# Selection of the sparse branch with two small operations per bit and new planner lengths; attention's two output parts stored apart

## The chip, the cores and the metric

The kernel runs on one core of a Trainium2 chip. A core has five engines with queues of their own: TensorE (PE in the profile; its weight loads are PEld), VectorE (DVE), ScalarE (ACT), GpSimd (POOL) and SyncE (SP), which here only starts transfers. The metric is the device time of one execution in microseconds (us).

## What is computed

One layer of a decoder trunk on 1024 tokens of width 1024. Three groups of 8 attention heads run side by side: A (sparse: an indexer scores all keys, each query keeps its 256 best), B (forgetting) and C (stick-breaking). Their outputs are projected, gated and summed, projected once more, and a layer norm, an MLP and a second layer norm follow. Cut to the two places of the change:

```python
score = einsum('bqhk,bqh->bqk', relu(dots), wb)          # indexer, 16 heads
score = where(causal, score, -inf)
_, idx = top_k(score, 256)                               # branch A: keys kept per query
...
branches = stack([o_a, o_b, o_c])                        # (3, b, s, 512)
up = einsum('ibsw,iwd->bsid', branches, w_branch)
merged = sum(up * sigmoid(gates), axis=2)
```

## The kernel before

Products of fp32 matrices are made from split operands: a tile is cut into a high and a low part, and three matmuls (high-high, high-low, low-high) give one product. In the first 1223 us the core makes the input projections and gates (`Dense`, whose results lie in three PSUM banks with the tag `d`), the indexer's scores, and then three times 8 heads of attention, in the order B (`Fox`), C (`Stick`), A (`Dsa`). A head has 4 units of two blocks of 128 queries; a unit makes its rows (`qk`), transposes the probabilities block by block (`tr`, 240 in all, 80 per branch; each ends on DVE with the subtraction `pl<-t,ph`) and multiplies them with the values (`pv`). Each `Stick` row needs a scan of the whole row on DVE (`u<-u,zero`).

**The selection.** `select` (L683) finds, for 6 blocks of 128 queries, the 256th largest score by bisection over the 32 bits of a float. For each bit DVE counts in each block how many scores reach the candidate (`count`, 6 operations `jk<-sc,fb` of 384 to 1024 columns) and then updates the candidate with operations on 128x6 values. After the last bit one more round counts, and 5 operations per block (`eq`, `rk`, `eq`, `eq`, `sc`; below "the ranking") turn the scores into distances or a large number for keys that are not kept. Branch A reads these.

**Who orders the work.** The program is written once, in an order that a planner chooses. `Plan.account` (L109) keeps a clock for each engine and adds to it the length that `_Engine` (L121) ascribes to each operation. `drive` (L753) emits the next piece of attention that is ready by these clocks, or else a step of the dense projections, which may run ahead of attention by two blocks of heads (`dense_upto`, L853). The selection is a generator that runs in the background: `fill_gap` (L95) emits pieces of it wherever DVE's planned clock has a gap of more than 0.8 us, up to a budget that grows with the transposes done (`bg_allowed`, L871), by the three numbers `BG`:

```python
while more and until - self.t["DVE"] > BG_GAP and self.bg_done < self.bg_allowed():
...
def bg_allowed():
    f = 3.0 * st["tr"] / len(trs)
    return BG[0] + (BG[1] - BG[0]) * f if f < 1.0 else BG[1] + (BG[2] - BG[1]) * (f - 1.0)
```

Each piece reports its length by `yield`, and the sum of these is `bg_done`. When the first rows of branch A come up and the selection isn't over, `next_attention` (L831) emits all that is left at once.

**The output of attention.** `Unit.pv` (L651) collects 512 queries of a head in one PSUM bank of 128 rows: 64 rows from the high and 64 from the low part of the values. ACT copies the two halves to SBUF, POOL adds them, and a transfer of 64x512 stores them to `o_scratch`. In the branch stage `load_o` (L890) brings 4 tiles of 128x1024 per branch back, and ACT and DVE split each.

Of the kernel before, what the change touches and what calls it, by code (L numbers as in the profile page):

```python
# [13 lines left out]
F32 = mybir.dt.float32  # L14
F32R = mybir.dt.float32r
BF16 = mybir.dt.bfloat16
I32 = mybir.dt.int32
# [28 lines left out]
FORGET = (13, 37)  # L46
X1_AT = 6


BG = (5.0, 95.0, 185.0)  # L50
BG_GAP = 0.8
# [69 lines left out]
class _Engine:  # L121
# [5 lines left out]
    def __getattr__(self, op):  # L127
        f = getattr(self.eng, op)

        def call(*args, **kw):  # L130
# [12 lines left out]
            if self.name == "T":  # L143
                eng, us = "PE", max(0.107, 0.000422 * n)
                if op == "matmul" and ins[0].dtype == BF16:
                    us = 0.056
            elif self.name == "V":
                fast = not psum and op in ("tensor_copy", "tensor_scalar") and "accum_out" not in kw
                eng, us = "DVE", 0.07 + n / (1920 if fast else 960)
            elif self.name == "A":  # L150
                eng, us = "ACT", (0.05 if psum else 0.09) + n / 1200
                if "accum_out" in kw:
                    us += 0.15
            elif self.name == "G":
                eng, us = "POOL", 0.06 + n * (0.0023 if op == "tensor_tensor" else 0.00106)
            else:
                size = n * out[0].shape[0] * 4
                eng, us, lat = "DMA", size / 340e3, 2.0
# [6 lines left out]
def trunk(ctx: ExitStack, tc: tile.TileContext, x, w_in, b_forget, w_branch, w_out,  # L165
# [269 lines left out]
    def gate(br, e):  # L435
        def evac(b):
            for c, t_ in zip(HALVES, b):
                g_ = plan.tile(dp, [P, 512], F32, tag="o", bufs=3, name="g_")
                A.activation(g_, t_, AF.Copy)
                nc.scalar.dma_start(g_dram[br, e * P:(e + 1) * P, c], g_)  # L440
        return proj_T([(0, win(OGT + br * D + e * P))], evac)
# [33 lines left out]
    def log_sigmoid():  # L475
        n = S * NH // P
        z, t1, t2 = (plan.tile(dp, [P, n], F32, tag="o", bufs=3, name=nm) for nm in ("z", "t1", "t2"))
        e_ = row_tile(7, "e_")[:, :n]
# [129 lines left out]
    class Unit:  # L608
# [42 lines left out]
        def pv(self, jp):  # L651
# [12 lines left out]
            if u % 2 == 1 and jp == u:  # L664
                t_ = plan.tile(dp, [P, 512], F32, tag="o", bufs=3, name="o")
                t2 = plan.tile(dp, [P, 512], F32, tag="o", bufs=3, name="o2")
                A.activation(t_[0:64], k.ob[0:64], AF.Copy)
                A.activation(t2[0:64], k.ob[64:128], AF.Copy)
                G.tensor_tensor(t_[0:64], t_[0:64], t2[0:64], ALU.add)

                q = nc.scalar if k.branch == 0 and h == NH - 1 else Q
                q.dma_start(o_dram[k.branch, h * HD:(h + 1) * HD, HALVES[u // 2]], t_[0:64])


    NI = len(TI)
    ub = cp.tile([P, NI], I32, name="ub")
    cb = cp.tile([P, NI], I32, name="cb")
    fb = cp.tile([P, NI], I32, name="fb")
# [4 lines left out]
    def select():  # L683
        def decode(dst, src):
            V.tensor_scalar(dst, src, 31, -1, op0=ALU.arith_shift_right, op1=ALU.bitwise_xor)
            V.scalar_tensor_tensor(dst, dst, -2 ** 31, src, op0=ALU.bitwise_or, op1=ALU.bitwise_xor)

        def count(cmp):
            for n, i in enumerate(TI):
                jk = plan.tile(ap, [P, S], U8, tag="jk", name="jk")  # L690
                V.tensor_scalar(jk[:, :(i + 1) * P], score[i], fb[:, n:n + 1].bitcast(F32), 0.0,
                                op0=cmp, op1=ALU.add, accum_out=cnt[:, n:n + 1])
                yield (i + 1) * 0.133

        for i in TI:
            G.affine_select(score[i][:, i * P:], score[i][:, i * P:], pattern=[[-1, P]],
                            compare_op=ALU.is_ge, fill=LOWEST, base=0, channel_multiplier=1)
        V.memset(ub, 0)
        for bit in range(31, -1, -1):
            V.tensor_scalar(cb, ub, (1 << bit) - (1 << 32 if bit == 31 else 0), None,  # L700
                            op0=ALU.bitwise_or)
            decode(fb, cb)
            yield from count(ALU.is_ge)
            V.tensor_scalar(mb, cnt, float(TOPK), None, op0=ALU.is_ge)
            V.copy_predicated(ub, mb, cb)
        decode(fb, ub)
        yield from count(ALU.is_gt)
        V.tensor_scalar(need, cnt, -1.0, float(TOPK), op0=ALU.mult, op1=ALU.add)

        for i in TI:  # L710
# [3 lines left out]
            eq = plan.tile(ap, [P, S], U8, tag="jk", name="eq")[:, :w]  # L714
            rk = plan.tile(dp, [P, S], F16, tag="o", bufs=3, name="rk")[:, :w]
            V.tensor_scalar(eq, score[i], thr, None, op0=ALU.is_equal)
            V.tensor_tensor_scan(rk, eq, zeros(P, w), 0.0, ALU.add, ALU.add)
            V.scalar_tensor_tensor(eq, rk, need[:, n:n + 1], eq, op0=ALU.is_le, op1=ALU.mult)
            V.scalar_tensor_tensor(eq, score[i], thr, eq, op0=ALU.is_le, op1=ALU.subtract)
            dist = plan.tile(dp, [P, S], F16, tag="o", bufs=3, name="dist")[:, :w]  # L720
            G.iota(dist, pattern=[[-1, w]], base=i * P, channel_multiplier=1,
                   allow_small_or_imprecise_dtypes=True)
            V.scalar_tensor_tensor(score[i], eq, BIG, dist, op0=ALU.mult, op1=ALU.add)
            yield (i + 1) * 0.7

# [164 lines left out]
    def load_o(n):  # L890
        parts = []
        for t_ in range(4):
            raw = gp.tile([P, S], F32, tag="oraw", bufs=3, name="oraw")
            Q.dma_start(raw, o_dram[branches[n], t_ * P:(t_ + 1) * P, :])
            parts.append((gp.tile([P, S], F32R, tag="oh", bufs=5, name="oh"),
                          gp.tile([P, S], F32R, tag="ol", bufs=5, name="ol")))
            split(*parts[-1], raw)
# [524 lines left out]
```

## Time and profile before

| | us |
|---|---|
| median of 3 runs (lowest, highest) | 2100.05 (2097.78, 2100.82) |
| the profiled execution | 2103.51 |
| its span, first to last instruction | 2101.8 |
| PE busy | 2026.3 (96%) |
| DVE busy | 1448.6 (69%) |
| ACT busy | 1054.0 (50%) |
| POOL busy | 541.5 (26%) |

The busy shares are over the whole span; the stretches that matter here are from 242 us (the first `pl<-t,ph` of attention) to 561 us (the first of branch C's transposes), from there to 862 us (near the end of branch C), from there to 1223 us (end of attention), and the branch stage up to 1420 us.

### The profile page before, as it was taken

Reading aid. Unit: us, or ns where it says so; the run is one execution under the profiler, and the core shown is the slowest. Engines: PE = TensorE matmul, PEld = TensorE weight load, DVE = VectorE, ACT = ScalarE, POOL = GpSimd, SP = SyncE. Lnnn points to the kernel's source line nnn. Section 1 sums busy time; section 2 is a strip of 40 time slices with the busy share of each in tenths; the row PEclk is TensorE's granted clock in tenths of the full one; section 3 lists DMA queues with packets and bytes.
Section 4 is the critical chain, followed back from the end, with each engine's and each line's share of the span. In section 5 each row is a group of like instructions: output and inputs, shape, how many; then the busy total and the mean of one; then the engine's idle time right before and its main releaser. Section 6 shows DMA issues by size and latency. Waiting matters only on the chain.

```text
span 2101.8 us, 29749 instructions
## 1 busy us (share of the span) xinstructions
PE 2026.3 (96%) x10534; PEld 1701.8 (81%) x10534; DVE 1448.6 (69%) x2651; ACT 1054.0 (50%) x2025; POOL 541.5 (26%) x508
## 2 busy tenths in 40 slices
PE   8999999999998998999999999999999999999998
PEld 7888878888877876888988888887787778888886
DVE  3886489788899999545433334766888776785557
ACT  5674455455565364446454443445544445654443
POOL 3212333333454356356445403100000000000003
PEclk9999999999999999999999999999999999999999
DMA  4111322232121221222122355631499945886653
GB/s 129 52 35 47 72 80 69 76 76 69 41 54 41 58 58 36 54 66 78 47 75 79 87 181 183 218 123 56 143 355 329 332 162 174 312 300 191 194 186 120
DMA packets 184277, 264.63 MB, mean 126 GB/s; under 512 B 17192, under 2 KB 109352, under 8 KB 182080
## 3 DMA queue, kind: packets, MB, share of 16 engines
q1 hardware_dynamic: 170144, 237.29, 36.7%
q10 hardware_dynamic: 13984, 25.43, 3.3%
q8 instruction: 83, 1.36, 0.3%
q14 instruction: 66, 0.54, 0.1%
HBM read 176.59 MB, written 73.50 MB: 119 GB/s over the span
## 4 chain that ended last, share of the span: by engine, by line
PE 59%; DVE 15%; DMA 8%; issue 5%; ACT 3%; POOL 1%; SPq 0%; DVEq 0%; ACTq 0%; POOLq 0%
PE d L137 49%; PE o L137 4%; DVE u L137 3%; PE l L137 3%; PE t L137 3%; DMA w2raw<-in_w_ff_dram 3%; DMA t_scratch<-w2raw 2%; DVE jk L137 2%; DVE pl L137 1%; DMA woraw<-in_w_out_dram 1%; DVE mr L137 1%; DMA w1raw<-in_w_ff_dram 1%; DVE w2raw L137 1%; DVE p L137 1%; DVE hl L137 1%
## 5 line engine op out<-in xcount | busy, mean ns | idle before, releaser
L137 PE MATMUL d<-xh,whi 128*128 128x512 f32 (+1 forms) x912 | 316.3, 401 | 17.5 <-DVE qb L137 12.8
L137 PE MATMUL d<-xh,wlo 128*128 128x512 f32 (+1 forms) x912 | 307.4, 393 | 0.0
L137 PE MATMUL d<-xl,whi 128*128 128x512 f32 (+1 forms) x912 | 303.2, 388 | 0.0
L137 PE MATMUL d<-u 128*128 128x512 f32 x1320 | 301.0, 390 | 1.9 <-ACT u L137 1.2
L137 PEld LDWEIGHTS d<-u 128*128 128x128 f32 x1320 | 247.5, 188 | 55.2 <-ACT u L137 2.2
L137 POOL TENSOR_TENSOR wlo<-wraw,whi 128x512 fp32r<-128x512 f32 x138 | 191.5, 1391 | 311.2 <-ACT whi L137 209.4
L137 POOL TENSOR_TENSOR z<-z,res 128x512 f32<-128x512 f32 x14 | 19.7, 1429 | 750.8 <-ACT z L137 747.9
L137 PEld LDWEIGHTS d<-xh,whi 128*128 128x128 f32 x912 | 168.4, 192 | 48.7 <-issue 18.0
L137 DVE TENSOR_TENSOR u<-sr,u 128x512 fp32r<-128x512 f32 x220 | 144.6, 702 | 89.9 <-ACT u L137 89.3
L137 ACT ACTIVATE u<-sr 128x512 fp32r<-128x512 f32 x220 | 130.2, 627 | 140.1 <-PE d L137 103.8
L137 PEld LDWEIGHTS d<-xl,whi 128*128 128x128 f32 x912 | 173.6, 191 | 31.8
L137 DVE TENSOR_TENSOR pl<-t,ph 128x512 fp32r<-128x512 f32 (+1 forms) x240 | 147.7, 630 | 67.0 <-ACT ph L137 65.7
L137 PEld LDWEIGHTS d<-xh,wlo 128*128 128x128 f32 x912 | 166.7, 191 | 27.1
L137 DVE TENSOR_SCALAR_CACHE_REDUCE jk<-sc,fb 128x384 uint8<-128x384 f32 (+2 forms) x198 | 186.2, 941 | 3.4
L137 ACT ACTIVATE whi<-wraw 128x512 fp32r<-128x512 f32 x136 | 86.1, 633 | 187.5 <-PE d L137 128.4
L137 ACT ACTIVATE p<-p,nm 128x128 f32<-128x128 f32 (+7 forms) x128 | 99.3, 776 | 142.4 <-DVE nm L137 129.7
L137 ACT ACTIVATE ph<-t 128x512 fp32r<-128x512 f32 (+1 forms) x240 | 128.0, 555 | 80.9 <-PE t L137 78.9
L137 PE MATMUL o<-pl,v 128*128 128x256 f32 x480 | 122.8, 292 | 20.5 <-DVE pl L137 20.3
L137 POOL TENSOR_SCALAR p<-p,sm 128x128 f32<-128x128 f32 (+7 forms) x128 | 96.1, 752 | 158.1 <-DVE sm L137 140.3
L137 PE MATMUL o<-ph,v 128*128 128x256 f32 x480 | 126.5, 284 | 0.4 <-ACT o L137 0.2
L137 PEld LDWEIGHTS o<-pl,v 128*128 128x128 f32 x480 | 92.2, 192 | 35.0 <-DVE pl L137 30.2
L137 ACT ACTIVATE mr<-mr 128x512 f32<-128x512 f32 x110 | 69.4, 631 | 93.5 <-DVE mr L137 91.8
(285 smaller groups left out, 4618.0 us busy)
## 6 DMA issues: line engine op xcount, KB each, us to landing
wraw<-in_w_in_dram SPq DMA_DIRECT2D x136, 256.0 KB, 2.9
sr<-h_scratch SPq DMA_DIRECT2D x112, 256.0 KB, 3.3
w1raw<-in_w_ff_dram SPq DMA_DIRECT2D x16, 1024.0 KB, 5.7
h_scratch<-mr SPq DMA_DIRECT2D x64, 256.0 KB, 2.4
w2raw<-in_w_ff_dram SPq DMA_DIRECT2D x16, 1024.0 KB, 8.2
t_scratch<-w2raw SPq DMA_DIRECT2D x16, 1024.0 KB, 7.8
sr<-t_scratch SPq DMA_DIRECT2D x64, 256.0 KB, 3.9
sg<-g_scratch SPq DMA_DIRECT2D x24, 512.0 KB, 3.3
```

The source lines that it names most:

```text
L137: r = f(*args, **kw)
```

## The change

It has three parts.

1. The candidate is kept in the form in which it is compared, so that a bit is updated by two operations (`mb`, then `fb`) in place of five (`mb`, `ub`, `cb`, `fb`, `fb`).
2. The planner's lengths for DVE change: operations of under 16 columns 0.2 us and more, scans about twice as long, operations with an accumulator 0.07 us longer. The pieces of the selection report other lengths too, and `BG` becomes (6, 115, 223).
3. The two parts of an attention output are copied in one ACT operation and stored apart by two transfers; POOL's addition goes. `load_o` fetches both parts, 8 tiles in place of 4 per branch (4 buffers, before 3), and DVE adds them ahead of the split.

```diff
-X1_AT = 6
-BG = (5.0, 95.0, 185.0)
+NO = 3
+BG = (6.0, 115.0, 223.0)
...
-                eng, us = "DVE", 0.07 + n / (1920 if fast else 960)
+                eng, us = "DVE", (0.2 if n < 16 else 0.07) + n / (1920 if fast else 960)
+                if op == "tensor_tensor_scan":
+                    us += n / 870
+                elif "accum_out" in kw or op == "tensor_tensor_reduce":
+                    us += 0.07
...
-                t_ = plan.tile(dp, [P, 512], F32, tag="o", bufs=3, name="o")
-                t2 = plan.tile(dp, [P, 512], F32, tag="o", bufs=3, name="o2")
-                A.activation(t_[0:64], k.ob[0:64], AF.Copy)
-                A.activation(t2[0:64], k.ob[64:128], AF.Copy)
-                G.tensor_tensor(t_[0:64], t_[0:64], t2[0:64], ALU.add)
+                t_ = plan.tile(dp, [P, 512], F32, tag="o", bufs=NO, name="o")
+                A.activation(t_, k.ob, AF.Copy)
                 q = nc.scalar if k.branch == 0 and h == NH - 1 else Q
-                q.dma_start(o_dram[k.branch, h * HD:(h + 1) * HD, HALVES[u // 2]], t_[0:64])
+                for part in range(2):
+                    q.dma_start(o_dram[k.branch, part, h * HD:(h + 1) * HD, HALVES[u // 2]],
+                                t_[64 * part:64 * part + 64])
...
-                yield (i + 1) * 0.133
+                yield (i + 1) * 0.134 + 0.13
...
-        V.memset(ub, 0)
+        V.memset(fb, 0)
         for bit in range(31, -1, -1):
-            V.tensor_scalar(cb, ub, (1 << bit) - (1 << 32 if bit == 31 else 0), None,
-                            op0=ALU.bitwise_or)
-            decode(fb, cb)
             yield from count(ALU.is_ge)
-            V.tensor_scalar(mb, cnt, float(TOPK), None, op0=ALU.is_ge)
-            V.copy_predicated(ub, mb, cb)
-        decode(fb, ub)
+            V.tensor_scalar(mb, cnt, float(TOPK), -1.0 if bit == 31 else float(1 << bit),
+                            op0=ALU.is_lt, op1=ALU.mult)
+            V.scalar_tensor_tensor(fb, fb, (1 << bit) >> 1, mb, op0=ALU.bitwise_xor, op1=ALU.bitwise_xor)
+            yield 0.5
...
-            yield (i + 1) * 0.7
+            yield (i + 1) * 1.05
...
-            raw = gp.tile([P, S], F32, tag="oraw", bufs=3, name="oraw")
-            Q.dma_start(raw, o_dram[branches[n], t_ * P:(t_ + 1) * P, :])
+            raw, raw2 = (gp.tile([P, S], F32, tag="oraw", bufs=4, name="oraw") for _ in range(2))
+            for part, r in enumerate((raw, raw2)):
+                Q.dma_start(r, o_dram[branches[n], part, t_ * P:(t_ + 1) * P, :])
+            V.tensor_tensor(raw, raw, raw2, ALU.add)
```

**The order that comes out of it.** New lengths make another order of the whole first 1223 us. Three places of it follow.

DVE at the turn from one bit to the next (`jk` a count, `sc` the scores of a block, `fb` the candidate that is compared), first before, then changed:

```order
L137 TENSOR_SCALAR jk_7931,cnt_102<-sc7_97,fb_100 128x1024
L137 TENSOR_SCALAR mb_101<-cnt_102 128x6
L137 COPY_PREDICATED ub_98<-mb_101,cb_99 128x6
L137 TENSOR_SCALAR cb_99<-ub_98 128x6
L137 TENSOR_SCALAR fb_100<-cb_99 128x6
L137 SCALAR_TENSOR_TENSOR fb_100<-fb_100,cb_99 128x6
L137 TENSOR_SCALAR jk_7938,cnt_102<-sc2_92,fb_100 128x384
```

```order
L137 TENSOR_SCALAR jk_7732,cnt_100<-sc7_97,fb_98 128x1024
L137 TENSOR_SCALAR mb_99<-cnt_100 128x6
L137 SCALAR_TENSOR_TENSOR fb_98<-fb_98,mb_99 128x6
L137 TENSOR_SCALAR jk_7736,cnt_100<-sc2_92,fb_98 128x384
L137 TENSOR_SCALAR jk_7738,cnt_100<-sc3_93,fb_98 128x512
```

Three of the five operations between two rounds of counts are gone.

DVE at the ranking of the last blocks, before in the midst of branch C (`u` its scans, `pl` the end of a transpose):

```order
L137 SCALAR_TENSOR_TENSOR u_8732<-u_8732,zero_66 128x768
L137 TENSOR_TENSOR pl_8760<-t_8755,ph_8759 128x384
L137 TENSOR_SCALAR eq_8780<-sc4_94,fb_100 128x640
L137 SCALAR_TENSOR_TENSOR rk_8781<-eq_8780,zero_66 128x640
L137 SCALAR_TENSOR_TENSOR u_8775<-u_8775,zero_66 128x896
L137 SCALAR_TENSOR_TENSOR eq_8780<-rk_8781,need_103,eq_8780 128x640
L137 TENSOR_TENSOR pl_8796<-t_8791,ph_8795 128x384
L137 SCALAR_TENSOR_TENSOR eq_8780<-sc4_94,fb_100,eq_8780 128x640
L137 TENSOR_TENSOR pl_8819<-t_8813,ph_8818 128x512
```

and changed, after the last scan of branch C (`v`, like `qa`, `qb`, `ka`, `kb`, empties a bank of a dense projection):

```order
L137 TENSOR_TENSOR v_9404<-d_9355,v_9404 128x4x64
L137 SCALAR_TENSOR_TENSOR sc6_96<-eq_8979,dist_8985 128x896
L137 TENSOR_TENSOR v_9405<-d_9355,v_9405 128x4x64
L137 TENSOR_SCALAR eq_8988<-sc7_97,fb_98 128x1024
L137 SCALAR_TENSOR_TENSOR rk_8989<-eq_8988,zero_66 128x1024
L137 SCALAR_TENSOR_TENSOR eq_8988<-rk_8989,need_101,eq_8988 128x1024
L137 TENSOR_TENSOR pl_9143<-t_9138,ph_9142 128x384
L137 SCALAR_TENSOR_TENSOR eq_8988<-sc7_97,fb_98,eq_8988 128x1024
L137 TENSOR_TENSOR pl_9152<-t_9146,ph_9151 128x512
L137 SCALAR_TENSOR_TENSOR sc7_97<-eq_8988,dist_8994 128x1024
```

Before, the ranking is spread over transposes 133 to 147 and its operations alternate with scans. Changed, all that is left of the selection at transpose 151 stands in one piece: 21 counts, 3 updates and the whole ranking, and between them only 2 scans, 8 `pl` and 14 operations that empty dense banks.

PE at the end of that piece, in the changed program (`o` the products with the values, of which each reads a `ph` and a `pl`; `d_9410` a dense projection):

```order
L137 MATMUL o_9121<-pl_9101,v_7557 128x256
L137 MATMUL o_9121<-ph_9142,v_7622 128x256
L137 MATMUL d_9410<-whi_9061,xl_81 128x256
...
L137 MATMUL d_9410<-whi_9196,xh_80 128x256
L137 MATMUL o_9121<-pl_9143,v_7622 128x256
L137 MATMUL o_9121<-ph_9142,v_7622 128x128
L137 MATMUL o_9121<-pl_9143,v_7622 128x128
L137 MATMUL t_9181<-ident_61,be_8861 128x128
```

The fifth row reads `pl_9143`, which on DVE stands behind all but two of the ranking's operations.

## Rows read from the trace of the kernel before

**Rows 1.** The page, busy us (share of the span) and instructions of each engine.
```profile
PE 2026.3 (96%) x10534; PEld 1701.8 (81%) x10534; DVE 1448.6 (69%) x2651; ACT 1054.0 (50%) x2025; POOL 541.5 (26%) x508
```

**Rows 2.** Busy time by stretch: start:end, length, then busy us (instructions), PEclk, DMA.
```profile
core 0: us, PE busy (x) PEld busy (x) DVE busy (x) ACT busy (x) POOL busy (x), PEclk, DMA share, GB/s
242.00:561.00 319.00, 311.25 (x1904) 267.99 (x1902) 265.50 (x718) 164.18 (x332) 114.09 (x116) 1.00 0.28 71
561.00:862.00 301.00, 271.10 (x1549) 225.20 (x1548) 282.32 (x391) 168.28 (x360) 152.11 (x111) 0.97 0.21 51
862.00:1223.00 361.00, 358.98 (x2112) 314.88 (x2111) 140.16 (x385) 177.93 (x357) 170.90 (x202) 1.00 0.26 70
1223.00:1420.00 197.00, 193.87 (x865) 159.76 (x864) 114.15 (x161) 85.67 (x123) 23.04 (x9) 1.00 0.54 181
```

**Rows 3.** Who PE waited for from 561 to 862 us: us, times, longest.
```profile
PE o L137 <- DVE pl L137: 15.9, 19, 2.3
PE d L137 <- DVE qb L137: 6.5, 4, 3.3
```

**Rows 4.** Groups by shape, DVE, 100 to 1220 us: the small operations (busy, mean ns).
```profile
L137 DVE TENSOR_SCALAR mb<-cnt 128x6 int32<-128x6 f32 x32 | 14.4, 448 | 0.4
...
L137 DVE COPY_PREDICATED ub<-mb,cb 128x6 int32<-128x6 int32 x32 | 10.2, 318 | 0.9
...
L137 DVE TENSOR_SCALAR cb<-ub 128x6 int32<-128x6 int32 x32 | 8.9, 279 | 1.0
...
L137 DVE TENSOR_SCALAR fb<-cb 128x6 int32<-128x6 int32 x32 | 8.7, 273 | 0.9
L137 DVE SCALAR_TENSOR_TENSOR fb<-fb,cb 128x6 int32<-128x6 int32 x32 | 8.1, 254 | 1.0
```

**Rows 5.** One tile's instructions: ns of one, lowest/median/highest, for the counts and for `mb`.
```profile
L137 DVE TENSOR_SCALAR_CACHE_REDUCE jk<-sc,fb x198: 598/938/1280, 184.5 to 773.8; 128x384 uint8<-128x384 f32 x33, 128x512 uint8<-128x512 f32 x33, 128x640 uint8<-128x640 f32 x33, 128x768 uint8<-128x768 f32 x33
```
```profile
L137 DVE TENSOR_SCALAR mb<-cnt x32: 153/172/1899, 205.4 to 749.0; 128x6 int32<-128x6 f32 x32
```

**Rows 6.** By stretch, the counts alone (each is two records on DVE).
```profile
184.00:561.00 377.00, 124.06 (x262) 1.00 0.27 69
561.00:862.00 301.00, 63.78 (x134) 0.97 0.21 51
```

**Rows 7.** By stretch, the ranking alone: DVE busy.
```profile
core 0: us, DVE busy (x), PEclk, DMA share, GB/s
561.00:862.00 301.00, 42.63 (x30) 0.97 0.21 51
```

**Rows 8.** A stretch in which PE ran matmuls of 512 columns alone.
```profile
1900.00:2000.00 100.00, 100.00 (x443) 82.84 (x442) 54.53 (x86) 42.71 (x74) 0.00 (x0) 1.00 0.64 195
```

**Rows 9.** Groups by shape, DVE, 561 to 862 us: a transpose's end, a scan, emptied banks.
```profile
L137 DVE TENSOR_TENSOR pl<-t,ph 128x512 fp32r<-128x512 f32 x43 | 28.8, 678 | 2.1 <-ACT ph L137 2.0
L137 DVE TENSOR_TENSOR_SCAN u<-u,zero 128x1024 f32<-128x1024 f32 x8 | 22.3, 2783 | 0.9 <-ACT u L137 0.9
...
L137 DVE TENSOR_TENSOR qb<-d,qb 64x512 fp32r<-64x512 f32 x8 | 5.6, 694 | 0.3
...
L137 DVE TENSOR_TENSOR v<-d,v 128x256 fp32r<-128x256 f32 x8 | 3.4, 420 | 1.4 <-ACT v L137 1.4
```

**Rows 10.** Groups by shape, DVE, 100 to 1220 us: two operations of the ranking.
```profile
L137 DVE TENSOR_SCALAR eq<-sc,fb 128x384 uint8<-128x384 f32 x1 | 1.5, 1507 | 0.0
...
L137 DVE TENSOR_SCALAR eq<-sc,fb 128x512 uint8<-128x512 f32 x1 | 0.5, 461 | 0.0
```

**Rows 11.** POOL's addition of the output parts, and SP's waits for it (us, times, longest).
```profile
L137 POOL TENSOR_TENSOR o<-o,o 64x512 f32<-64x512 f32 x48 | 66.7, 1389 | 79.6 <-ACT o L137 67.5 <-issue 11.5 <-PE l L137 0.4
```
```profile
SPq L137 <- POOL o L137: 290.0, 44, 18.0
```

**Rows 12.** Branch stage, by tile: the split of fetched outputs, their landing, POOL's sum.
```profile
L137 DVE TENSOR_TENSOR ol<-oraw,oh x12: 1219/1226/1226, 1226.5 to 1319.3; 128x1024 fp32r<-128x1024 f32 x12
...
DMA to landing us min/median/max: 3.6/4.7/8.6
```
```profile
L137 POOL TENSOR_TENSOR mr<-mr,sg x8: 2713/2720/2737, 1281.5 to 1321.8; 128x1024 f32<-128x1024 f32 x8
```

More of the change, by code (lines that the diff above doesn't have):

```diff
@@ L437, in evac @@
             for c, t_ in zip(HALVES, b):
-                g_ = plan.tile(dp, [P, 512], F32, tag="o", bufs=3, name="g_")
+                g_ = plan.tile(dp, [P, 512], F32, tag="o", bufs=NO, name="g_")
                 A.activation(g_, t_, AF.Copy)
@@ L476, in log_sigmoid @@
         n = S * NH // P
-        z, t1, t2 = (plan.tile(dp, [P, n], F32, tag="o", bufs=3, name=nm) for nm in ("z", "t1", "t2"))
+        z, t1, t2 = (plan.tile(dp, [P, n], F32, tag="o", bufs=NO, name=nm) for nm in ("z", "t1", "t2"))
         e_ = row_tile(7, "e_")[:, :n]
@@ L664, in pv @@
             if u % 2 == 1 and jp == u:
-                t_ = plan.tile(dp, [P, 512], F32, tag="o", bufs=3, name="o")
-                t2 = plan.tile(dp, [P, 512], F32, tag="o", bufs=3, name="o2")
-                A.activation(t_[0:64], k.ob[0:64], AF.Copy)
-                A.activation(t2[0:64], k.ob[64:128], AF.Copy)
-                G.tensor_tensor(t_[0:64], t_[0:64], t2[0:64], ALU.add)
+                t_ = plan.tile(dp, [P, 512], F32, tag="o", bufs=NO, name="o")
+                A.activation(t_, k.ob, AF.Copy)
                 q = nc.scalar if k.branch == 0 and h == NH - 1 else Q
-                q.dma_start(o_dram[k.branch, h * HD:(h + 1) * HD, HALVES[u // 2]], t_[0:64])
+                for part in range(2):
+                    q.dma_start(o_dram[k.branch, part, h * HD:(h + 1) * HD, HALVES[u // 2]],
+                                t_[64 * part:64 * part + 64])
     NI = len(TI)
-    ub = cp.tile([P, NI], I32, name="ub")
-    cb = cp.tile([P, NI], I32, name="cb")
     fb = cp.tile([P, NI], I32, name="fb")
@@ L683, in select @@
     def select():
-        def decode(dst, src):
-            V.tensor_scalar(dst, src, 31, -1, op0=ALU.arith_shift_right, op1=ALU.bitwise_xor)
-            V.scalar_tensor_tensor(dst, dst, -2 ** 31, src, op0=ALU.bitwise_or, op1=ALU.bitwise_xor)
         def count(cmp):
@@ L714, in select @@
             eq = plan.tile(ap, [P, S], U8, tag="jk", name="eq")[:, :w]
-            rk = plan.tile(dp, [P, S], F16, tag="o", bufs=3, name="rk")[:, :w]
+            rk = plan.tile(dp, [P, S], F16, tag="o", bufs=NO, name="rk")[:, :w]
             V.tensor_scalar(eq, score[i], thr, None, op0=ALU.is_equal)
@@ L719, in select @@
             V.scalar_tensor_tensor(eq, score[i], thr, eq, op0=ALU.is_le, op1=ALU.subtract)
-            dist = plan.tile(dp, [P, S], F16, tag="o", bufs=3, name="dist")[:, :w]
+            dist = plan.tile(dp, [P, S], F16, tag="o", bufs=NO, name="dist")[:, :w]
             G.iota(dist, pattern=[[-1, w]], base=i * P, channel_multiplier=1,
@@ L1406 @@
     o = nc.dram_tensor("out_0_dram", (1, S, D), F32, kind="ExternalOutput").ap()
-    o_dram = nc.dram_tensor("o_scratch", (3, NH * HD, S), F32, kind="Internal").ap()
+    o_dram = nc.dram_tensor("o_scratch", (3, 2, NH * HD, S), F32, kind="Internal").ap()
     g_dram = nc.dram_tensor("g_scratch", (3, D, S), F32, kind="Internal").ap()
```

## The prediction

> **What bounds the kernel now.** I read the busy shares first: PE is busy for 96% of the span [rows 1], so only its idle time and its slow clock can be won. Next comes the busy time by stretch, to see where these lie [rows 2]. From 561 to 862 us, in the stick-breaking branch, PE is idle for 301 - 271.1 = 29.9 us and its granted clock is 0.97, which is some 9 us more. DVE is busy for 282.3 of the 301 us (94%) there. The stretch ahead of it loses 319 - 311.25 = 7.8 us at full clock with DVE at 83%, the one behind it 2.0 us with DVE at 39%. So DVE's load in branch C is the bound that can be moved, worth 39 us at the most. The waits of that stretch say the same: PE waits for `pl`, the end of a transpose, and for `qb`, the emptying of a dense bank [rows 3], both on DVE.
>
> The idle share is one measure of that loss. In PE's weight loads the same three stretches read 84%, 75% and 87% [rows 2]; if the third is full speed, the second lost 301 x (1 - 0.748/0.872) = 43 us. The Trainium skill (Perfetto Trace Analysis, Identifying the Most-Contended Engine) holds busy matmul time for a poor measure and weight loads for the better one; by it the loss is 43 us and the sum below 4 us lower. I stay with 39, which needs no assumption that the two stretches mix matmuls alike.
>
> **Small operations.** Per bit `ub`, `cb` and one `fb` go: 10.2 + 8.9 + 8.7 = 27.8 us of DVE over 32 bits, plus a little for the last decoding; `mb` and an operation like `fb<-fb,cb` stay, 14.4 + 8.1 = 22.5 us [rows 4]. Of what goes, 96 operations at the 172 ns that is usual [rows 5] would be 16.5 us; the rest is waiting, since `mb` takes up to 1899 ns while a count of 1024 columns never takes over 1280. PE sees this saving only where DVE is late.
>
> **Where the selection lies.** By the order, 131 counts stood ahead of transpose 81 before, and 122 do now; 55 follow up to transpose 151, and 21 stand in the closing piece. Before, the 561 to 862 stretch held 67 counts at 63.8/67 = 0.95 us [rows 6], 11 updates, and the ranking with 42.6 us [rows 7]. Now the part of branch C ahead of the closing piece loses the ranking (42.6), 12 counts (11.4), and of the updates some 12 us: 11 updates of five operations were 17 us by the means of [rows 4], 9 of two are 6 us, and a last decoding goes. DVE falls from 282 to about 216 us.
>
> PE's work there, at full pace, was 301 - 39 = 262 us. By the order 16 us of dense matmuls move from here behind transpose 151, so 246 us remain. DVE to PE is then 216/246 = 0.88, where the stretch from 242 to 561 has 265.5/311 = 0.85 and loses 2.4% [rows 2]. I take that share, 6 us, so **33 us are won**; the bounds are 39 and, if half of the stalls stay because each row still needs a scan of up to 2.8 us [rows 9] between `qk` and its product, 20.
>
> **From 242 to 561 us** DVE loses 9 counts (8.5 us) and 64 of 99 small operations (about 20 us at 50.3/160 = 0.31 us each [rows 4]). DVE falls to 237 of 319 us. Two lumps of 29 and 24 counts now stand at the places where dense work piles up, so I take half of the 7.8 us: **4 us won**, bounds 0 and 8.
>
> **The closing piece** is what the change adds. From its first count to the last write of scores, DVE does 21 counts (20.0), 3 updates (3 x 0.70 = 2.1), the ranking (42.6), 8 `pl` (5.4), 8 operations like `qb` (5.6), 6 `v` (2.5) and 2 scans (at most 5.6) [rows 4, 6, 7, 9]: 84 us. PE has between the same points 74 matmuls of 512 columns and 187 of 256, and 55 short ones. At 100/443 = 0.226 us per 512 columns [rows 8] and half of it for the others that is 44 us. More dense work can't come: the rule of two blocks ahead stops it, and three `d` banks, which DVE must empty between rank operations, hold it back. So PE is short by up to 40 us. The ranking's lengths are not its own: an `eq` of 384 columns took 1507 ns and one of 512 took 461 [rows 10], so the first waited some 1.16 us. If 11 of the 30 did as much, the ranking alone is 30 us, an estimate, which makes the piece 71 us and the shortfall 27. **I take 27 us lost**, the end nearer to what holds then: POOL, whose additions are the likely cause of such waits, has no output parts to add any more (66.7 us over the program [rows 11]) and few products of branch C. The bounds are 40, and 10, if PE stands only at the last stop, where `pl_9143` waits for the last block's ranking (42.6 x 1024/4608 columns = 9.5 us).
>
> **POOL, ACT and SP in attention.** 48 additions of 1.39 us leave POOL, which bounds nothing. SP waited 290 us for them in 44 waits [rows 11], with weight fetches queued behind. The store now waits for ACT's one copy, so what is behind it starts earlier; 48 more issues come on SP, of under half a microsecond each as SP's stores of that shape show, which its idle time hides. I cost this at nothing; if the cover went, a fetch would be late by an issue, under 1 us.
>
> **Branch stage.** 12 more fetches of 512 KB and 12 more DVE operations. An addition is nearest to `ol` with 1.23 us [rows 12], together 15 us beside DVE's 114 of 197 [rows 2]: hidden. For the first branch the path from the last store to the first product gets one addition longer (1.2 us), but by the order 17 us more dense work is left to cover it. DMA is at 0.54 of its time; 12 transfers with a landing of 4.7 us [rows 12] delay others a little. **1 us lost**; bounds 0 and 8, two late first tiles.
>
> **Sum.** -33 - 4 + 27 + 1 = -9 us. The profiled execution took 2103.5 us, so 2094.5; the median of the runs shown lies 3.5 us under it, so 2091.0. Under 0.2% (4.2 us) can't be told from no change.
>
> **Rivals.**
> - *The closing piece costs all of its bound.* The ranking keeps its 42.6 us and PE stands for 40 us, and its clock falls as it did at a rate of 9 us per 30 us idle [rows 2], 12 us more. Then -33 - 4 + 52 + 1 = +16: 2116, slower. It decides from 36 us for the piece on. For it: DVE's fixed order puts `pl_9143` behind the ranking. Against: POOL is calmer then. Chance 0.2, of which a part lies below 2113.
> - *The dense work covers the piece.* Only 10 us are lost: 33 + 4 - 10 - 1 = 26 won, 2074. For it: the matmuls are there, and the planner's lengths now have DVE's scans nearly right. Against: the banks. Chance 0.22.
> - *The stalls of branch C stay half.* -20 - 4 + 27 + 1 = +4: 2104, no change. For it: a scan of 2.8 us lies on each row's path whatever the load. Chance 0.18.
> - *The new additions wait for POOL.* In the second branch POOL's `mr` sums hold for 2.72 us each [rows 12]. If 4 additions wait for one each ahead of a first product, 11 us are lost there, the sum is +1 and the time 2101. All 12 `ol` took 1219 to 1226 ns, so none waited. The Trainium skill (SBUF — State Buffer, Who interferes with whom) says that a DVE operation with two inputs in SBUF blocks against a GpSimd operation that reads SBUF, while `tensor_scalar` with an accumulator doesn't; the counts' steady times agree, no row shows it for the additions. Chance 0.03.
>
> My forecast has 0.37. Faster by over 0.2% (under 2095.9): the second rival and nearly all of the forecast, 0.55. Within 0.2%: the third, the fourth and edges, 0.22. Slower: the first and the third's upper side, 0.23. The range goes from 2072, just under the second rival, to 2113, within the first.
>
> **What would show it.** Right: from the first `pl` of branch C to the closing piece PE's idle share is near 2 to 3% and its clock 1.00; the closing piece is a stretch of 70 to 80 us with DVE at 100% and PE idle or waiting for `pl`, `qb` and `v` for some 27 us; the whole `mb` group under 14 us; no gap in front of the first product of each branch. Wrong: PE idle in branch C as before (the new lengths did not help), a closing piece that costs over 36 us or under 15, or PE waiting in the branch stage for `ol`.

## The result, and the profile after

The change takes 2077.04 us (median of 4 runs, 2074.55 to 2080.84) against 2100.16 (4 runs, 2097.78 to 2100.82): a ratio of 0.9889, interval 0.9875 to 0.9904, so 23 us faster. The forecast was 9 us, with 2091 us and a range that holds the result. The profiled execution took 2076.87 us, its span is 2075.2.

The page, busy time of each engine, to be held against [rows 1]:

```profile
PE 2019.2 (97%) x10534; PEld 1699.6 (82%) x10534; DVE 1433.7 (69%) x2565; ACT 1020.5 (49%) x1977; POOL 473.0 (23%) x460
```

PE has as many instructions as before and 7 us less busy time; 86 operations are gone from DVE and 48 from POOL. Next the windows of the changed kernel, columns as in [rows 2]: branch B up to the first transpose of C; from there to the first count of the closing piece; the closing piece; the rest of attention; the branch products.

```profile
244.80:556.80 312.00, 309.53 (x1902) 268.88 (x1901) 242.93 (x639) 152.74 (x316) 93.45 (x100) 0.99 0.30 79
556.80:795.30 238.50, 231.26 (x1399) 194.83 (x1398) 210.59 (x288) 144.87 (x320) 109.09 (x83) 1.00 0.25 63
795.30:866.20 70.90, 57.65 (x356) 51.38 (x354) 69.01 (x105) 20.96 (x41) 21.70 (x20) 0.88 0.18 45
866.20:1178.80 312.60, 312.30 (x1806) 271.33 (x1805) 133.35 (x374) 154.44 (x317) 142.09 (x178) 1.00 0.30 77
1178.80:1338.90 160.10, 159.44 (x707) 131.82 (x706) 94.40 (x111) 65.94 (x79) 24.55 (x10) 1.00 0.69 227
```

Ahead of the closing piece PE is now idle for 7.2 of 238.5 us at full clock, with DVE at 88%. The closing piece is there, 70.9 us long with DVE at 97%; PE is idle in it for 13.2 us, and its mean clock is 0.88. What the clock costs is read from the stretches in which it stood at the lower of its two levels (0.50, 1.2 GHz). In the closing piece these are two; they begin 0.4 us after a stop of 2.3 us and 1.3 us after one of 3.6:

```profile
810.99:824.64 13.65, 8.41 (x28) 6.78 (x27) 13.15 (x29) 1.19 (x2) 1.97 (x3) 0.50 0.40 96
858.78:862.19 3.41, 2.90 (x12) 2.60 (x12) 3.38 (x2) 1.13 (x2) 3.41 (x2) 0.50 0.30 64
```

PE worked for 11.3 of these 17.1 us. At this level matmuls of 512 columns started every 0.43 us, in place of 0.23 [rows 8], so half of the 11.3 us are lost: 5.7, and with the idle time 18.9. (A loss taken from the mean clock, 12% of 70.9 us, would count idle time at the lower level twice.)

To compare the two kernels over the same work I cut branch C from its first to past its last transpose (the 81st to the 161st `pl<-t,ph`). Between these points PE has the same number of instructions in both. The windows of before, and of the change:

```profile
560.90:906.20 345.30, 314.45 (x1847) 264.90 (x1846) 297.00 (x427) 187.94 (x399) 168.51 (x129) 0.97 0.20 51
```
```profile
556.80:885.20 328.40, 307.77 (x1847) 261.69 (x1846) 287.93 (x415) 176.71 (x383) 140.68 (x113) 0.97 0.23 60
```

Branch C is 16.9 us shorter. Of that, 10.2 us are PE's idle time (30.9 to 20.6) and 6.7 us its busy time, with 1847 matmuls in both. Most of the 6.7 us is the clock, though its mean is the same. Before, six stretches of this cut stood at the lower level, and PE worked through nearly all of them; after, it is the two of the closing piece, and a third of their time was idle anyway. The sum of the six:

```profile
sum 20.47, PE 20.22 PEld 16.88 DVE 20.31 ACT 6.77 POOL 9.84; mean PE 3.37 PEld 2.81 DVE 3.38 ACT 1.13 POOL 1.64
```

Half of 20.2 and of 11.3 us are 10.1 and 5.7 us lost, so 4.5 of the 6.7 us are the clock. With that taken off, the matmuls come to 304.3 and 302.1 us, and 2.2 us are left.

Branch B, cut at the first and the 81st `pl`, went from 318.9 to 312.0 us. From the 161st `pl` to the last branch product it is 455.7 and 453.8 us. These three give 25.7 of the 26.6 us between the two spans (more than the 23 us between the medians, since the execution traced before lies 3.4 us over its median). The rest is noise of stages that nobody touched: the first product of the MLP, unchanged, took 326.8 to 336.1 us in the 14 traces of this study (334.1 before, 330.2 after), which is why verdicts below go by medians and traces by intervals of equal work.

Who PE waited for in branch C, in the same cut, after ([rows 3] is before):

```profile
PE d L137 <- DVE qb L137: 8.3, 3, 5.2
PE o L137 <- DVE pl L137: 5.8, 8, 2.3
PE o L137 <- ACT o L137: 3.6, 1, 3.6
```

and in the closing piece alone:

```profile
PE d L137 <- DVE qb L137: 5.2, 1, 5.2
PE o L137 <- DVE pl L137: 4.0, 3, 2.3
PE o L137 <- ACT o L137: 3.6, 1, 3.6
```

PE's longest stop was for a dense bank that DVE had to empty. The stop that I took for the main one, the product of `pl_9143`, cost 1.1 us. The stop of 3.6 us goes back to DVE as well: it was for ACT's copy of an output, and ACT had stood still for a `v` of DVE and then for the ranking's `sc`:

```profile
855.85 0.38 ACT L137 ACTIVATE v<-d 128x256 fp32r<-128x256 f32 x1 [5.36 <-DVE v L137]
856.85 0.60 ACT L137 ACTIVATE o<-o 128x512 f32<-128x512 f32 x1 [0.61 <-DVE sc L137]
```

The ranking, and the two small operations per bit, after ([rows 7] and [rows 4] are before):

```profile
184.00:900.00 716.00, 32.20 (x30) 0.99 0.27 68
```
```profile
L137 DVE TENSOR_SCALAR mb<-cnt 128x6 int32<-128x6 f32 x32 | 9.0, 281 | 0.4
...
L137 DVE SCALAR_TENSOR_TENSOR fb<-fb,mb 128x6 int32<-128x6 int32 x32 | 7.0, 218 | 1.0
```

The ranking fell from 42.6 to 32.2 us for the same 30 operations, and the small ones from 50.3 to 16.0 us.

### The profile page after: what moved, and what is told of

Read it like the earlier page. It is cut to its first block, busy times and chain, and to the rows that moved or that the text cites. A ratio compares the mean times of both kernels' runs of the same rounds, so it can differ in the third digit from the quotient of the medians.

```text
span 2075.2 us, 29623 instructions
## 1 busy us (share of the span) xinstructions
PE 2019.2 (97%) x10534; PEld 1699.6 (82%) x10534; DVE 1433.7 (69%) x2565; ACT 1020.5 (49%) x1977; POOL 473.0 (23%) x460
## 4 chain that ended last, share of the span: by engine, by line
PE 64%; DVE 13%; DMA 7%; issue 4%; ACT 2%; POOL 1%; SPq 0%; DVEq 0%; ACTq 0%; POOLq 0%
PE d L137 52%; PE o L137 5%; PE l L137 4%; PE t L137 4%; DVE u L137 2%; DMA w1raw<-in_w_ff_dram 2%; DMA t_scratch<-w2raw 2%; DVE jk L137 2%; DVE mr L137 1%; DMA w2raw<-in_w_ff_dram 1%; DMA woraw<-in_w_out_dram 1%; DVE w2raw L137 1%; DVE pl L137 1%; DVE eq L137 1%; DVE hl L137 1%
## 5 line engine op out<-in xcount | busy, mean ns | idle before, releaser
L137 PE MATMUL d<-xh,whi 128*128 128x512 f32 (+1 forms) x912 | 315.4, 400 | 17.3 <-DVE qb L137 14.7
L137 DVE TENSOR_TENSOR_SCAN u<-u,zero 128x128 f32<-128x128 f32 (+3 forms) x64 | 109.9, 1723 | 18.7 <-ACT u L137 17.2
```

Source lines behind the costliest of these rows:

```text
L137: r = f(*args, **kw)
```

## The experiments

"Small" is part 1 of the change, "plan" part 2, "apart" part 3. The table holds the medians of all eight combinations; each ratio is to the kernel before, run on the same chip in the same session.

| parts | us | ratio [95%] |
|---|---|---|
| none | 2099.3 to 2100.2 | |
| small | 2090.86 | 0.9956 [0.9939, 0.9972] |
| apart | 2092.82 | 0.9969 [0.9956, 0.9982] |
| plan | 2099.95 | 1.0002 [0.9991, 1.0014] |
| small, apart | 2081.96 | 0.9915 [0.9898, 0.9933] |
| small, plan | 2087.89 | 0.9943 [0.9926, 0.9959] |
| apart, plan | 2087.95 | 0.9948 [0.9929, 0.9967] |
| all three | 2077.04 | 0.9889 [0.9875, 0.9904] |

**Each part alone.** Small alone, planned anew with the old lengths:

```diff
-            V.tensor_scalar(cb, ub, (1 << bit) - ...)
-            decode(fb, cb)
...
-            V.tensor_scalar(mb, cnt, float(TOPK), None, op0=ALU.is_ge)
-            V.copy_predicated(ub, mb, cb)
+            V.tensor_scalar(mb, cnt, float(TOPK), ..., op0=ALU.is_lt, op1=ALU.mult)
+            V.scalar_tensor_tensor(fb, fb, (1 << bit) >> 1, mb, ...)
```

> The kernel before with the two small operations per bit alone; the planner's lengths and budget, and the outputs' addition on POOL, stay. The order theory (the gain comes from where the planner puts the selection): DVE's load in branch C is still in the same places, so 0 to -6 us. The work theory (the gain is DVE time saved): 28 us of DVE less, and branch C, where DVE is 94% busy, gives most of its share back, -12 to -18 us. The POOL theory (the gain comes from the additions that left POOL): 0.

Measured: 2090.86 us, 8.4 under its kernel before, between the order theory and the work theory. In the traces branch B takes 312.2 us (318.9 before) and branch C 338.5 (345.2): the gain lies where DVE does the selection, half of it in B. (These 13.4 us are more than the 8.4 of the medians; the trace of before is of a long execution.)

Apart alone:

```diff
-                A.activation(t_[0:64], k.ob[0:64], AF.Copy)
-                A.activation(t2[0:64], k.ob[64:128], AF.Copy)
-                G.tensor_tensor(t_[0:64], t_[0:64], t2[0:64], ALU.add)
+                A.activation(t_, k.ob, AF.Copy)
...
+            V.tensor_tensor(raw, raw, raw2, ALU.add)
```

> The kernel before with the output parts stored apart alone. Order theory: 0 to -3 us, plus up to 3 lost in the branch stage. Work theory: 0. POOL theory: -10 to -20 us, with the small operations and the ranking on DVE clearly shorter (mb mean under 250 ns, ranking under 35 us in place of 44).

Measured: 2092.82 us, 6.4 less, for the part that the forecast had at nothing. That is less than the POOL theory gave, and its two signs failed: over the program `mb` still takes 397 ns in the mean (448 before), and the ranking 40.9 us (42.6). The cut of branch C in that run:

```profile
558.80:900.20 341.40, 312.68 (x1847) 264.13 (x1847) 288.74 (x427) 178.04 (x383) 145.78 (x113) 0.97 0.23 57
```

DVE has the same 427 records there as before and 8.3 us less busy time (297.0 before), though nothing was taken from DVE in this stretch.

Plan alone:

```diff
-BG = (5.0, 95.0, 185.0)
+BG = (6.0, 115.0, 223.0)
...
-                eng, us = "DVE", 0.07 + n / (1920 if fast else 960)
+                eng, us = "DVE", (0.2 if n < 16 else 0.07) + n / (1920 if fast else 960)
...
-            yield (i + 1) * 0.7
+            yield (i + 1) * 1.05
```

> The kernel before with the planner's lengths and budget alone (five small operations, POOL adds). Order theory: -12 to -20 us, PE idle in branch C ahead of the closing piece under 10 us. Work theory and POOL theory: 0 to -5 us, and DVE over 90% busy there still.

Measured: 2099.95 us, no change (0.9991 to 1.0014). Its windows, branch B, branch C up to the 850 us mark, and the last 42 us with the ranking:

```profile
242.70:562.70 320.00, 312.31 (x1902) 268.13 (x1901) 253.52 (x696) 163.67 (x332) 114.00 (x115) 1.00 0.27 70
562.70:848.50 285.80, 265.74 (x1578) 224.53 (x1577) 253.50 (x383) 168.08 (x361) 138.05 (x108) 0.98 0.22 55
848.50:890.10 41.60, 31.30 (x200) 28.35 (x200) 40.62 (x51) 9.99 (x22) 17.30 (x14) 0.87 0.11 27
```

PE is idle for 20.1 us and then 10.3 us more: moving DVE's work to the end of branch C alone moves PE's stops with it. The order theory failed here: the move by itself, to which with the small operations the forecast gave 33 us won against 27 lost, is a wash.

**Two parts of three.** Small with apart, old planner; then the change without apart; then the change without small. Each takes over the edits shown above and leaves the third out:

```diff
-BG = (6.0, 115.0, 223.0)
+BG = (5.0, 95.0, 185.0)
```

> The whole change without the planner's part: two small operations and outputs apart, old lengths and budget. Order theory: -3 to -8 us. Work theory: -12 to -18 us. POOL theory: -10 to -20 us. If this reaches -23 us, the planner's part gives nothing.

Measured: 2081.96 us, 17 less than before, within the ranges of the work theory and the POOL theory and beyond the order theory's 8. By the medians the plan is worth 4.9 us on top of the other two; the intervals of this run and of the whole change (0.9898 to 0.9933, 0.9875 to 0.9904) overlap a little.

```diff
-                A.activation(t_, k.ob, AF.Copy)
+                A.activation(t_[0:64], k.ob[0:64], AF.Copy)
+                A.activation(t2[0:64], k.ob[64:128], AF.Copy)
+                G.tensor_tensor(t_[0:64], t_[0:64], t2[0:64], ALU.add)
```

> The changed kernel with the outputs added on POOL as before, planned (parts one and two of the change). If the parts add up as they did in the old order (-9 and -6.5 us): 2083 to 2086. If the planner's part needs a free POOL: 2088 or more, near the small operations alone.

Measured: 2087.89 us, above what adding up would give. Apart is worth 10.9 us on top of the other two; that this is more than the 6.4 alone is not clear of noise.

```diff
-            V.scalar_tensor_tensor(fb, fb, (1 << bit) >> 1, mb, ...)
+            V.copy_predicated(ub, mb, cb)
...
+            decode(fb, cb)
```

> The changed kernel with the five operations per bit of the kernel before: outputs apart and the new planner lengths only, planned anew (116 counts ahead of transpose 81 in place of 122, 24 in the closing piece in place of 21). Theory 1: the small operations cost only their own DVE time, as three idle ones per bit did (2081.7): 2081 to 2085 us. Rival: the new lengths are worth nothing without them, since the closing piece grows by what the small operations take there and ahead of it; then the time is that of outputs apart in the old order, 2090 to 2094 us.

Measured: 2087.95 us, between the two expectations: small is worth 10.9 us on top of the others. In every pair of rows of the table that differ in one part, small brings 8.4 to 12, apart 6.4 to 12, and the plan nothing alone but 3 to 5 by the medians once DVE is relieved. The plan's three gains agree in sign, but the intervals of each pair overlap.

**Small, with the order nearly held.** Three idle operations of 128x6 per bit, put into the changed kernel behind `mb` without the planner's knowledge. In the trace 83 of PE's 10534 instructions and 46 of DVE's other 2565 stand at another place than in the change:

```diff
+            for _ in range(3):
+                nc.vector.tensor_scalar(xb, mb, 1, None, op0=ALU.bitwise_or)
```

> The changed kernel with three idle operations of 128x6 per bit put back on DVE behind the planner's back (they read mb and write a tile that nobody reads), so the order stays nearly the changed kernel's. Work theory (DVE time itself): the 9 us that the small operations gave in the old order come back, +6 to +10 us over the changed kernel, 2083 to 2087. Order theory: +0 to +3, since in the new order DVE has room ahead of the closing piece.

Measured: 2081.71 us (0.9913 [0.9898, 0.9927]), 4.7 over the change and between the two theories; the two intervals overlap by 0.0006. The 96 operations took 28.0 us of DVE, nearly what the removed ones took (27.8 [rows 4]):

```profile
L706 DVE TENSOR_SCALAR xb<-mb 128x6 int32<-128x6 int32 x96 | 28.0, 292 | 0.9
```

Branch C grows from 328.3 to 332.3 us, while B doesn't (312.0 and 310.5). So DVE's time in small operations costs time in branch C; that they cost less here than by the table is no contradiction, since the planned kernel without them also places its counts otherwise.

**Apart, with the order held.** The changed kernel with a POOL addition of zeros behind each output copy; the store waits for it. PE's and DVE's order stays that of the change. Then the same with 64x16 values, so that the wait stays and nearly all of POOL's work goes:

```diff
+                nc.gpsimd.tensor_tensor(t_[0:64], t_[0:64], zero[:64].to_broadcast([64, 512]), ALU.add)
```

> The changed kernel with an addition of 64x512 on POOL put back behind each copy of an output (it adds zeros to the first part), unplanned, so order and transfers stay as they are; the first part's store waits for it. If POOL's additions and the stores' wait for them are what outputs apart saved: +4 to +8 us, ranking and mb longer, SP waiting some 200 us or more for POOL o. If the saving came by the other order that the planner made of it: 0 to +2.

```diff
+                nc.gpsimd.tensor_tensor(t_[0:64, 0:16], t_[0:64, 0:16], zero[:64].to_broadcast([64, 16]), ALU.add)
```

> The changed kernel with a POOL addition of zeros behind each output copy, like the run that put POOL's 64x512 addition back (2083.4 us), but on 64x16 values only; the store still waits for it. The order of PE and DVE is that of the changed kernel. Theory P: what the addition costs is POOL's time (48 x 1.4 us in an in-order queue, behind which stand branch C's row products, for which a transpose and a bank wait): with a tenth of that work the time is that of the changed kernel, 2076 to 2078.5 us, and SP still shows waits for POOL. Theory W: what it costs is that the store, and whatever stands behind it on SP, waits for POOL's turn: then 2081 to 2084 us, as with the large addition.

Measured: 2083.37 us with the large addition (0.9930 [0.9911, 0.9950]), 2077.94 with the small one (0.9897 [0.9874, 0.9920]). The two intervals overlap (0.9911 to 0.9920), but every run with the large addition (2080.60 to 2089.07) took longer than every run with the small one (2077.28 to 2080.07), the medians stand on the two sides that the expectation set apart, and the traces agree. Of the signs that the first expectation named, the waits of some 200 us on SP and a longer `mb` didn't come (6.3 us, 9.0 in the change), and the ranking grew only to 33.6 us. SP's waits for POOL, first with the large, then with the small addition:

```profile
SPq L137 <- POOL o L672: 62.8, 43, 5.6
```
```profile
SPq L137 <- POOL o L672: 48.1, 25, 9.7
```

The store still waits for 48 us in all with the small one, and no time clear of noise is lost by it. Branch C, cut as above, with the large and the small addition:

```profile
553.40:890.60 337.20, 308.29 (x1847) 262.05 (x1846) 295.13 (x415) 176.86 (x383) 161.65 (x129) 0.98 0.23 58
```
```profile
553.40:883.60 330.20, 307.63 (x1847) 262.30 (x1846) 288.61 (x415) 176.95 (x383) 150.41 (x129) 0.97 0.24 59
```

With the large addition branch C is 7.0 us longer than with the small one and 8.8 longer than in the change (328.4); branch B (310.5 in both) and branch A don't differ. DVE has the same 415 records in all three and is busy for 295.1, 288.6 and 287.9 us. Which operations grew, the scans `u<-u,zero` of the two runs say, in the same cut (DVE busy):

```profile
553.40:890.60 337.20, 113.34 (x61) 0.98 0.23 58
```
```profile
553.40:883.60 330.20, 107.94 (x61) 0.97 0.24 59
```

In the change they take 105.5 us, so the large additions lengthen the scans by 7.9 us, while the 152 records of the counts stay at 72.3 in both. Scans are on the path of every row of branch C. PE's waits for `pl`, and for a bank from which ACT makes a row (`be`), rise from 5.5 and 1.1 us with the small addition to 10.0 and 3.9 with the large:

```profile
PE o L137 <- DVE pl L137: 10.0, 9, 3.1
...
PE l L137 <- ACT be L137: 3.9, 5, 1.0
```

The traces show single collisions. Below, the large addition and then a product of a row (`be`) stand beside a scan of 128x128, which takes 2.89 us (1.45 in the other run); then a small addition that came 1.56 us after the start of a scan ends with it:

```profile
597.70 2.89 DVE L137 TENSOR_TENSOR_SCAN u<-u,zero 128x128 f32<-128x128 f32 x1 [0.87 <-ACT u L137]
597.32 1.03 POOL L672 TENSOR_TENSOR o<-o,zero 64x512 f32<-64x512 f32 x1
598.32 1.99 POOL L137 TENSOR_TENSOR be<-be,u 128x1023 f32<-128x1023 f32 x1
```
```profile
593.55 3.74 DVE L137 TENSOR_TENSOR_SCAN u<-u,zero 128x1024 f32<-128x1024 f32 x1 [0.32 <-ACT u L137]
595.11 2.20 POOL L672 TENSOR_TENSOR o<-o,zero 64x16 f32<-64x16 f32 x1
```

The two runs have the same 2565 DVE instructions in the same order. One by one in branch C, nine scans are over 300 ns longer with the large addition, six of them beside such an addition, and one is 1.45 us shorter. All DVE instructions together are 6.5 us longer, while DVE's idle time stays (42.1 and 41.6 us). So DVE wasn't late by waiting for POOL's own queue, in which the products of the rows stand behind the additions: its work itself took longer. A second way isn't separated from it: ACT's waits for those products rose too, from 23.3 to 29.7 us, and PE's wait of 3.9 us for `be` may come from there.

Both engines hold each other up: POOL's large addition takes 1029 ns at the least and up to 3019 in this run. The Trainium skill (SBUF — State Buffer, Who interferes with whom) says that a DVE instruction with two inputs in SBUF contends with a GpSimd instruction that reads SBUF, that the one which comes first has the ports to its end, and that one with at most one such input, outside its two-port modes, doesn't. The scans and the counts stand as it says. `mb`, with one input, took up to 1896 ns in the change, beside a product of POOL; whether it runs in a two-port mode no run shows. What lengthens need not be the scans: in the order of before, taking the additions out left the scans nearly alone (101.0 us to 100.0 from 500 to 900 us), and it was `mb` (10.5 to 6.1 us there), other small operations and a little the ranking whose time fell.

**The closing piece, more and less of it.** Three budgets in the changed kernel, no other edit. First a later one, with 36 counts in the closing piece (21 in the change):

```diff
-BG = (6.0, 115.0, 223.0)
+BG = (6.0, 95.0, 185.0)
```

> The changed kernel with the budget (6, 95, 185): 101 counts ahead of transpose 81 (122 in the change), and 36 counts and the whole ranking in the closing piece (21 in the change). Theory 1: the closing piece costs by its length, since PE has a fixed 44 us or so of work beside it and no more can come: 15 more counts at 0.95 us are 14 us more of DVE alone, and the stretches ahead can give back at most 5 of them, as they lose only some 10 us as it is: 2084 to 2091 us. Rival: load moved along DVE's queue is a wash, what the piece loses the stretches ahead win, as the planner's part alone showed (2100 against 2099): 2075 to 2080 us.

Measured: 2088.63 us (0.9947 [0.9929, 0.9965]), 11.6 over the change. Its closing piece:

```profile
804.50:894.90 90.40, 72.13 (x380) 61.52 (x381) 87.84 (x152) 19.88 (x40) 30.72 (x25) 0.84 0.18 44
```

PE is idle for 18.3 us, and of the rest 23.1 us are at the lower clock, which loses 11.5 more: 29.8 against 18.9, 11 us for 15 counts. Now two earlier budgets:

```diff
-BG = (6.0, 115.0, 223.0)
+BG = (20.0, 140.0, 240.0)
```

> The changed kernel with the budget (20, 140, 240): 141 counts ahead of transpose 81 in place of 122, and the ranking between transposes 145 and 154, so no closing piece of 20 counts and ranking at transpose 151. If the closing piece's price (about 17 to 20 us) is what eats the planner's gain, and the stretch ahead of it stays at DVE's 88%: -8 to -14 us, 2063 to 2069. If the load only comes back into branch C: 2074 to 2080.

Measured: 2072.42 us (0.9870 [0.9849, 0.9890]), between the two expectations: 141 counts stand ahead of transpose 81 and the ranking at transposes 145 to 154. This is the best median of all, 4.6 under the change, though the intervals overlap.

```diff
-BG = (6.0, 115.0, 223.0)
+BG = (40.0, 150.0, 240.0)
```

> The changed kernel with the budget (40, 150, 240): 151 counts ahead of transpose 81 (122 in the change), all counts done by transpose 129, the ranking at transposes 129 to 151, no closing piece. Theory 1 (the piece's loss of 17 to 22 us can be won where the load is spread thinly enough): the stretch of branch B then has DVE near 85% and loses about 8 us in place of 2.5, branch C has the ranking again, at 200 of 238 us, and loses about 10 to 12 in place of 7, and the piece's 20 us are gone: 2066 to 2071 us, at or under the 2072.4 of the budget (20, 140, 240). Rival (what DVE must do beside attention costs the same wherever it stands): 2075 to 2080 us.

Measured: 2074.26 us (0.9879 [0.9854, 0.9903]), above what the first theory gave and under its rival. Its windows, branch B, branch C up to the ranking, and the ranking:

```profile
243.00:552.70 309.70, 307.83 (x1900) 266.75 (x1899) 247.03 (x653) 152.75 (x316) 93.38 (x99) 1.00 0.31 79
552.70:735.10 182.40, 177.39 (x1089) 151.74 (x1088) 159.71 (x232) 110.04 (x242) 82.63 (x63) 1.00 0.24 61
735.10:828.90 93.80, 81.14 (x443) 66.67 (x441) 85.03 (x77) 49.20 (x104) 49.92 (x35) 0.95 0.24 65
```

Branch B takes 29 counts more than in the change and loses only 1.9 us. But where the ranking stands, PE again is idle for 12.7 us and loses 3.9 by its clock: 16.6 against the 18.9 of the closing piece. Spreading the counts is worth 3 to 5 us by the medians, which is not clear of noise. Nor is the price of the ranking the same in either place: in the closing piece PE's idle time was 7.5 us beside the counts and 5.7 beside the ranking (32.2 us of DVE), here 12.7 in a stretch in which the ranking (39.5 us) alternates with branch C's rows.

## Why the prediction was right or wrong, point by point

- **The bound.** Right in place: the gain lies in branches B and C, where DVE does the selection. "Worth 39 us at the most" was read from idle time and clock; in the cut of equal work these fell from 41.0 to 26.3 us, which is 14.7 of the 16.9 won. The other 2.2 are matmuls that took less time at full clock. The weight loads, by which the sum would have come out 4 us lower, come nearer to the result. The Trainium skill (Perfetto Trace Analysis, Identifying the Most-Contended Engine) holds their busy time for the better measure than that of matmuls. The two traces agree: with the lower clock taken off as above, the weight loads of this cut come to 256.5 and 257.0 us, the matmuls to 304.3 and 302.1.
- **The small operations.** The step "PE sees this saving only where DVE is late" was right, but it was then used as a term of DVE's average load alone. Small alone brought 8.4 us, with the ranking still in the midst of branch C.
- **Branch B.** 4 us forecast with bounds 0 and 8, measured 6.9.
- **Ahead of the closing piece.** 6 us of loss at a DVE share of 0.88 forecast; 7.2 us at 0.88 measured. Right.
- **The closing piece.** This step failed in size: "that is 44 us" of PE's work beside the piece, and so "27 us lost". The length was right (71 us forecast, 70.9 measured), but PE had 356 matmuls there in place of 316, and was at work for 57.7 us, or 52.0 at full clock. So 18.9 us were lost, of which I hadn't thought 5.7 to be the clock, and the main stop was not `pl_9143` but a bank. That 36 counts cost 11 us more shows the mechanism: the piece costs by its length. The ranking came out as estimated (30 us, measured 32.2), but not for the first reason given, that POOL has no output parts to add: with the additions on POOL it took 33.3 us (the change without apart) and 33.6 (additions put back), and without them in its old place 40.9. In all runs it took 40.9 to 44.0 us where the old planner puts it, 32.2 to 37.4 in a closing piece, and 35.5 and 39.5 with the two earlier budgets, which spread it again; so it was mainly its place that decided. The lower bound of 10 us was worked out with 4608 columns for six blocks that have 4224; with these it is 10.3 in place of 9.5.
- **POOL, ACT and SP in attention.** This step failed too, and as a mechanism: "48 additions of 1.39 us leave POOL, which bounds nothing", "I cost this at nothing". It was worth 6.4 us alone, 10.9 on top of the other two parts, and 5.4 between the two runs that keep the order and the store's wait and differ in POOL's work. What I had priced, the store's wait, was indeed worth nothing. What I left out is that POOL's additions lengthen DVE's operations, and DVE was the bound that I had just named; I used the same contention for the ranking's lengths and didn't carry it over to this step.
- **Branch stage.** +1 us forecast; with branch A before it 1.9 us less measured. The 12 additions took 1210 to 1227 ns, so none was held up. One of the 12 `ol` took 3433 ns (1216 at the least), but PE waited for none. Right.
- **The sum.** By equal work, branch C was forecast at -33 + 27 = -6 and gave -16.9, B -4 and gave -6.9, the rest +1 and gave -1.9. Of the 17 us that were missed 11 lie in branch C: 8.1 are the closing piece at 18.9 in place of 27, 2.2 the matmuls at full clock, and under 1 the stretch ahead of it. By runs instead of terms, the run with apart left out took 332.6 us in branch C, so that 4.3 us there go to apart when planned (8.8 when the additions are put back with the order held), and as much in branch B (316.3 in place of 312.0). The two accounts overlap, and no run divides the one by the other.
- **The rivals.** None took place as it was told. The closing piece didn't cost all of its bound, because the ranking shrank and PE had more work beside it. It wasn't covered by the dense work either, since the banks stopped it; that the result lies 3 us from that rival's 2074 is luck, as the piece lost 18.9 us and not 10. That the range holds the result is luck in part, too, since it got there by a term that was priced at nothing. What the planner moves is a wash by itself, which no rival had said; had the change been its second part alone, the result would have been "no change".

What stays open: why the plan is worth nothing alone and 5 us with the rest. By the medians it is so (each single pair's intervals overlap), and PE's stops move with DVE's work; that it needs a DVE with slack ahead of the piece is only argued.

## What to carry to other kernels

An engine that "bounds nothing" can still cost time through the one that does: before work is taken from POOL or left there at no price, look which operations of the bound engine run beside it, and how far their longest times stand above their shortest. When work is only moved along the queue of the bound engine, expect its waits to move with it, and look for work to take off instead. Compare two kernels over stretches with the same instructions of PE, and take off what its clock costs stretch by stretch: idle time alone missed 6.7 of 16.9 us, and a mean clock that was the same in both hid that 4.5 of them were the clock.

## What was not expected of the hardware

- The same 1847 matmuls of branch C showed a busy time of 314.45 us before and 303.84 (1846 of them) in the run with the budget (20, 140, 240). At full clock that is 304.3 and 301.1 us, so most of it was the clock. PE's weight loads (1846 in both, 264.90 and 259.30 us) come to 256.5 and 257.0 at full clock: of the two, they are nearer to a constant of the work.
- A POOL addition of 64x16 took 206 ns at the least and 2198 at the most, one of 64x512 from 1029 to 3019: both were held up by up to 2 us, whatever their size, as the smallest operations of DVE were (`mb` still 139 to 1896 ns after the change). The five additions of 64x16 that took over 2 us all ended within 10 ns of the end of a scan on DVE that had begun before them.
- PE's clock fell to a mean of 0.88 and 0.84 in closing pieces in which PE was still busy for 81 and 80% of the time; that cost 5.7 and 11.5 us, two fifths and three fifths as much again as the idle time itself.
